# An encoder's MLP input: the last quarter turned by VectorE and transfers instead of TensorE

## Chip, cores and metric

The kernel runs on one core of a Trainium2 chip. The metric is the device time in microseconds of one execution; the median of three runs is taken.

## The reference, cut to what matters

Two layers; each has attention heads, an output projection that is added to the residual `h` (256 tokens x 2048), and an MLP. All arithmetic is float32.

```python
h = h + concatenate([mix, cross], axis=-1) @ w_o[i]          # 2048 -> 2048
n = rms_norm(h, mlp_norm[i])
h = h + square(relu(n @ w_up[i])) @ w_down[i]                # 2048 -> 8192 -> 2048
```

The up product needs the normed input with its features on the partitions, while `h` has tokens on the partitions. So the MLP's input must be transposed: 16 blocks `k` of 128 features by 256 tokens.

## The kernel before

**Exactness.** Each float32 operand is split into a rounded part hi and the rest lo (`split`, L505: ScalarE writes hi at L507, VectorE writes lo at L508), and a product is three matmuls: hi by hi, hi by lo, lo by hi (`products`, L399, the matmul at L411, 256 tokens as the moving side).

**Order.** The program is a list of grains, each one a step of TensorE with stages `load`, `lift`, `pre`, `prep` that are written some grains ahead (`ahead`). Within an engine the order is set afterwards by a planner that simulates the timeline. `tc.issue_after(ins)` puts the instructions of a block that go to the engine of `ins` behind it on that engine; `past(fn, pair)` does so for a ScalarE and a VectorE instruction; `later(n, ...)` writes a piece n grains later. Every engine and each DMA queue runs in order.

**Output projection and MLP input.** The projection comes in four blocks of 512 columns. After each of the first three, `o_done` adds it to `h`; after the third it takes a provisional scale from three quarters of the squares (`guard`), and quarters 0 to 2 of the MLP's input (4 blocks `k` each) go this way: ScalarE scales (`scaled`, L962), VectorE transposes 32 x 32 blocks within the partitions (`far_blocks`, L626), four transfers on SP's queue move the blocks to their partitions (L629, 128 KB each), and `arrived` applies the gain and splits (`split_pair`: ScalarE L537, VectorE L538) into `hT`. The last quarter can be finished only when the fourth block of the projection is summed: L1005 adds its two PSUM tiles to the scaled residual `y` (`begun`), and TensorE transposes `y` in eight 128 x 128 pieces (`transposed`, L525, matmuls with the identity into `pt_n`), from which L537 and L538 write `hT`. `box["ready"]` is the last pair of them; the add of the fourth block to `h` (L985) comes behind it.

**The up stage.** `up_grains` makes one chunk `m` of 128 of the 8192 columns: a 1 MB load into `raw_U` (L1045, two buffers, SP's queue), and two halves of eight `k` each, split apart (tiles `uh`, `ul`, two buffers). The first four chunks (`LEAD`) come before the first down product, so 4 x 48 = 192 matmuls. Numbering the halves 0 to 7, halves 2 and 4 lie in `u_b` (tag `b`, three buffers, shared with the down weights), half 5 in `u_th`, `u_tl` (later the down product's `th`, `tl`), the others in `uh`, `ul`. Before, the four chunks run one after the other, each with all of its 16 `k`. Halves of chunks 1 and 2 are written behind `box["summed"]`, the last sum of L1005. The chunks' sums lie in the PSUM pool `acc` of four banks, which the projection's last tiles use too. `squared` follows each chunk.

**The first down step** loads `b` (L1154, SP), and its lift copies a piece into a tile `t` of tag `T` (two buffers; ScalarE L1165), adds by a GpSimd transfer (L1166), and VectorE adds three more (L1172 to L1174); `th`, `tl` are split from it. `h_s`, the scaled quarter 2, and `y` are in tag `T` too.

## Time and profile before

| | |
|---|---|
| median of three runs | 1991.65 us (1991.28 to 1991.91) |
| the profiled execution | 1992.31 us, span 1990.5 us |
| TensorE clock granted | 0.999 of full speed |
| first up matmul to first down matmul, layer 0 | 419.24 to 442.84 us |
| the same, layer 1 | 1323.35 to 1346.07 us |

Times inside the profile count from the start of the span. PE is TensorE, PEld its weight loads, DVE VectorE, ACT ScalarE, POOL GpSimd, and SPq, POOLq are the instructions that issue transfers. A timeline row has the start, the duration (merged over the count at its end), engine, line, operation, written and read tiles; in brackets is the idle time before it and what ended that. A group's row ends with busy time, mean ns of one, and the idle time before. Matmuls are pipelined, so that the duration of one is longer than the slot that it takes; the chain of waits gives the slots.

### The profile page before, as it was taken

The numbers are of one execution on the slowest core, as the hardware profiler recorded it, in microseconds if no ns is written. First come the engines' busy times: TensorE is split into PE (matmuls) and PEld (weight loads), VectorE is DVE, ScalarE is ACT, GpSimd is POOL, SyncE is SP. The second block draws the span as 40 slices with busy tenths as digits, with TensorE's granted clock in tenths as the row PEclk, the third lists the DMA queues.
The fourth block names the chain that finished last, engine by engine and source line by source line (L and its number), as shares of the span: only waits on it lengthen the run. The fifth ranks groups of instructions, "written<-read, shape, count | busy, mean of one in ns | idle before, by whom it ended". The sixth has DMA issues, their size and how long they took to land.

```text
span 1990.5 us, 33096 instructions
## 1 busy us (share of the span) xinstructions
PE 1980.6 (100%) x12832; PEld 1799.3 (90%) x12832; DVE 1725.6 (87%) x2096; ACT 1442.2 (72%) x2105; POOL 149.9 (8%) x205
## 2 busy tenths in 40 slices
PE   9999999999999999999999999999999999999998
PEld 8999999899999999999998888889999999999997
DVE  6777767589999999999999879779999999999997
ACT  6755555577887778877887657668788777877786
POOL 0000000000000000000001001000000000000001
PEclk9999999999999999999999999999999999999999
DMA  7855655767777777777778765667777777777775
GB/s 289 320 193 208 199 192 184 271 198 248 222 231 237 229 232 237 222 239 235 222 229 223 267 221 171 220 202 249 238 222 229 236 229 229 237 229 241 228 225 156
DMA packets 110685, 452.46 MB, mean 227 GB/s; under 512 B 18880, under 2 KB 40640, under 8 KB 63168
## 3 DMA queue, kind: packets, MB, share of 16 engines
q1 hardware_dynamic: 90144, 413.38, 60.7%
q0 software_dynamic: 20096, 36.45, 10.5%
q8 instruction: 100, 1.64, 0.3%
q10 hardware_dynamic: 288, 0.52, 0.1%
q14 instruction: 57, 0.47, 0.1%
HBM read 397.78 MB, written 4.19 MB: 202 GB/s over the span
## 4 chain that ended last, share of the span: by engine, by line
PE 97%; ACT 1%; DVE 1%; DMA 1%; issue 0%; DVEq 0%; SPq 0%; POOLq 0%; POOL 0%; ACTq 0%
PE ps_u L411 35%; PE p L1195 10%; PE p L1199 10%; PE p L1198 10%; PE ps_s L411 9%; PE ps_m L391 7%; PE ps_m L392 7%; PE ps_m L388 7%; DMA first<-in_x 0%; ACT sq L856 0%; PE sc_ps L604 0%; PE sc_ps L605 0%; PE sc_ps L603 0%; PE av L696 0%; PE av L697 0%
## 5 line engine op out<-in xcount | busy, mean ns | idle before, releaser
L411 PE MATMUL ps_u<-hT,uh 128*128 128x256 f32 x3874 | 674.6, 276 | 0.0
L411 PEld LDWEIGHTS ps_u<-hT,uh 128*128 128x128 f32 x3874 | 588.5, 188 | 5.8
L411 PE MATMUL ps_u<-hT,ul 128*128 128x256 f32 x1994 | 550.7, 276 | 0.0
L507 ACT ACTIVATE uh<-raw_U 128x1024 fp32r<-128x1024 f32 x262 | 277.6, 1061 | 153.8 <-PE ps_u L411 150.7
L411 PEld LDWEIGHTS ps_u<-hT,ul 128*128 128x128 f32 x1994 | 374.3, 188 | 0.0
L507 ACT ACTIVATE hi<-raw 128x1024 fp32r<-128x1024 f32 (+1 forms) x215 | 222.0, 1036 | 182.2 <-PE ps_m L392 93.3
L508 DVE TENSOR_TENSOR lo<-raw,hi 128x1024 fp32r<-128x1024 f32 (+1 forms) x215 | 255.3, 1191 | 109.2 <-ACT hi L507 108.5
L508 DVE TENSOR_TENSOR ul<-raw_U,uh 128x1024 fp32r<-128x1024 f32 x262 | 319.8, 1221 | 14.2 <-ACT uh L507 14.1
L508 DVE TENSOR_TENSOR tl<-t,th 128x2048 fp32r<-128x2048 f32 x120 | 274.8, 2290 | 51.1 <-ACT th L507 50.9
L507 ACT ACTIVATE th<-t 128x2048 fp32r<-128x2048 f32 x120 | 230.9, 1924 | 90.4 <-PE p L1199 90.4
L508 DVE TENSOR_TENSOR bl<-b,bh 128x1536 fp32r<-128x1536 f32 x120 | 210.3, 1753 | 0.3 <-ACT bh L507 0.3
L1166 POOL DMA_DIRECT2D t<-b x120 | 104.2, 868 | 1159.3 <-ACT t L1165 1103.4
L1195 PE MATMUL p<-th,a_s 128*128 128x512 f32 x480 | 187.4, 391 | 0.0
L1198 PE MATMUL p<-tl,a_s 128*128 128x512 f32 x480 | 187.2, 390 | 0.0
L1199 PE MATMUL p<-th,a_s 128*128 128x512 f32 x480 | 186.7, 389 | 0.0
L507 ACT ACTIVATE bh<-b 128x1536 fp32r<-128x1536 f32 x120 | 178.7, 1489 | 3.5
L411 PE MATMUL ps_s<-nT,hi 128*128 128x256 f32 x896 | 154.6, 277 | 0.0
L1199 PE MATMUL p<-bh,a_s 128*128 128x512 f32 x360 | 140.9, 391 | 0.0
L1198 PE MATMUL p<-bl,a_s 128*128 128x512 f32 x360 | 140.1, 389 | 0.0
L1195 PE MATMUL p<-bh,a_s 128*128 128x512 f32 x360 | 140.1, 389 | 0.0
L411 PEld LDWEIGHTS ps_s<-nT,hi 128*128 128x128 f32 x896 | 135.3, 188 | 0.2
L411 PE MATMUL ps_s<-nT,lo 128*128 128x256 f32 x448 | 124.2, 277 | 0.0
(293 smaller groups left out, 3639.2 us busy)
## 6 DMA issues: line engine op xcount, KB each, us to landing
raw_U<-in_w_up SPq DMA_DIRECT2D x128, 1024.0 KB, 6.3
b<-in_w_pair SPq DMA_DIRECT2D x120, 1024.0 KB, 5.8
raw<-in_w_o SPq DMA_DIRECT2D x32, 1024.0 KB, 4.9
t<-b POOLq DMA_DIRECT2D x120, 256.0 KB, 6.5
raw<-in_w_b SPq DMA_DIRECT2D x21, 1024.0 KB, 5.5
raw<-in_w_av SPq DMA_DIRECT2D x12, 1024.0 KB, 5.1
raw<-in_w_aq SPq DMA_DIRECT2D x12, 1024.0 KB, 4.9
raw<-in_w_ak SPq DMA_DIRECT2D x12, 1024.0 KB, 4.9
```

Of the source, the lines that this page charges most:

```text
L388: first = nc.tensor.matmul(ps, ah, hi[:, s], start=st, stop=False)
L391: nc.tensor.matmul(ps, ah, lo[:, s], start=False, stop=False)
L392: final = nc.tensor.matmul(ps, al, hi[:, s], start=False, stop=sp)
L411: ins = nc.tensor.matmul(ps, x, acts[:, k, part], start=k == n == 0, stop=k == KT - 1 and n == 2)
L507: first = nc.scalar.activation(dst_hi, src, AF.Copy)
L508: return first, nc.vector.tensor_tensor(dst_lo, src, dst_hi.bitcast(F32), op=ALU.subtract)
L1166: nc.gpsimd.dma_start(s[:, 3, :], b[:, 1, :], accum_op=ALU.add)
L1195: ins = nc.tensor.matmul(ps, a[:, 0, ai, :], hi[:, s], start=entered, stop=False, skip_group_check=True)
L1198: nc.tensor.matmul(ps, a[:, 0, ai, :], lo[:, s], start=False, stop=False, skip_group_check=True)
L1199: nc.tensor.matmul(ps, a[:, 1, ai, :], hi[:, s], start=False, stop=ends, skip_group_check=True)
```

## The change

In both layers, `far_blocks` with the new `summed` replaces `transposed` for the last quarter: VectorE sums a tile and turns it, twice, and four transfers on SP's queue bring the blocks. The target is `y` and the blocks lie in `box["still"]`, the scaled quarter 2. `box["summed"]` is now the second of these transposes.

Chunks 0, 1 and 2 first do their `k` 0 to 11, and their last quarters follow chunk 2's third, in the order 0, 1, 2; then chunk 3 with all 16. Chunk 2's sum goes to the PSUM pool `att`. Halves 6 and 7 get rooms of their own (`u_z`), which are the later tiles `z0`, `z1`, now opened with the first down step. Half 2 is written earlier and no longer behind the sums; chunk 2's halves are written behind the last split before them.

```diff
@@ products
+        return ins
@@ far_blocks
-            nc.vector.transpose(blocks[:, :, i].rearrange("p b k j -> p k b j"),
-                                src(i).rearrange("p (k n b) -> p k b n", k=4, b=4))
+            box["turned"] = nc.vector.transpose(blocks[:, :, i].rearrange("p b k j -> p k b j"),
+                                                src(i).rearrange("p (k n b) -> p k b n", k=4, b=4))
@@ arrived
-            split_pair(dst, raw[:, :, :, n], which, k0 + n, by_quarters=True)
+            last = split_pair(dst, raw[:, :, :, n], which, k0 + n, by_quarters=True)
+        return last
@@ o_done, scaled
+            box["still"] = y
@@ o_done, nb == 3
-                for i in range(NT):
-                    box["summed"] = nc.vector.scalar_tensor_tensor(y[:, i, :], w.ps[i], box["scale"][:, i : i + 1],
-                                                                   y[:, i, :], op0=ALU.mult, op1=ALU.add)
-                box["ready"] = transposed(box["hT"], lambda i, k: y[:, i, k % 4 * P : (k % 4 + 1) * P],
-                                          list(range(12, KT)), (G_M0, G_M1)[layer])
+                def summed(i):
+                    nc.vector.scalar_tensor_tensor(y[:, i, :], w.ps[i], box["scale"][:, i : i + 1], y[:, i, :],
+                                                   op0=ALU.mult, op1=ALU.add)
+                    return y[:, i, :]
+
+                raw = far_blocks(summed, (box["still"], y.rearrange("p t c -> p (t c)")))
+                box["summed"] = box["turned"]
+                box["ready"] = arrived(box["hT"], raw, 12, (G_M0, G_M1)[layer])
@@ up_grains, prep and prepared
-            with tc.issue_after(box["summed"].ins) if m in (1, 2) else nullcontext():
+            if m == 2:
+                past(lambda: prepared(hf), box["splits"][-1])
+                return
+            with tc.issue_after(box["summed"].ins) if m == hf == 1 else nullcontext():
                 prepared(hf)
...
-            if lead and (half in (2, 4) or half > 4 and half % 3 == 2):
+            if lead and half in (2, 4, 5, 6, 7):
...
+                elif half > 5:
+                    room = at.mlp.tile([P, 2, HALF], F32R, tag=f"z{hf}", name="u_z")
+                    own[hf] = room[:, 0], room[:, 1]
@@ up_grains, run
-                box["z"] = [at.mlp.tile([P, 4, 512], F32, tag=f"z{q}", name=f"z{q}") for q in range(2)]
-                box["z_set"] = set()
...
-                    own["ps"] = at.acc.tile([P, 512], F32, tag="acc", name="ps_u")[:, :SEQ]
+                    pool, tag, bufs = (at.att, "att", at.banks) if m == 2 else (at.acc, "acc", None)
+                    own["ps"] = pool.tile([P, 512], F32, tag=tag, bufs=bufs, name="ps_u")[:, :SEQ]
...
+            acts = box["hT0" if lead else "hT"]
+            if m < 3 and hf == 1:
+                hi, lo = own.pop(hf)
+                last = products(own["ps"], acts, KT // 2, KT // 4, hi, lo)
+                box.setdefault("rests", []).append((m, own["ps"], hi[:, HALF // 2 :], lo[:, HALF // 2 :]))
+                if m == 2:
+                    for other, ps, hi, lo in box.pop("rests"):
+                        with tc.issue_after(last.ins):
+                            last = products(ps, acts, KT * 3 // 4, KT // 4, hi, lo)
+                        squared(layer, other, ps)
+                return
...
-            squared(layer, m, own["ps"])
-
-        soon = (8, 8, 3) if m == 1 else SOONER
+            if m > 2:
+                squared(layer, m, own["ps"])
+
+        early = (8, 8, 6)
-        return [Grain(lambda: run(0), None, load, None, lambda: prep(0), soon),
-                Grain(lambda: run(1), after, None, None, lambda: prep(1), SOONER)]
+        return [Grain(lambda: run(0), None, load, None, lambda: prep(0), early if m < 2 else SOONER),
+                Grain(lambda: run(1), after, None, None, lambda: prep(1), early if m == 0 else SOONER)]
@@ down_grains, run, first step
+                box["z"] = [at.mlp.tile([P, 4, 512], F32, tag=f"z{q}", name=f"z{q}") for q in range(2)]
+                box["z_set"] = set()
```

More of the change, by code (lines that the diff above doesn't have):

```diff
@@ L1090, in run @@
                 if lead:
-                    own["ps"] = at.acc.tile([P, 512], F32, tag="acc", name="ps_u")[:, :SEQ]
+                    pool, tag, bufs = (at.att, "att", at.banks) if m == 2 else (at.acc, "acc", None)
+                    own["ps"] = pool.tile([P, 512], F32, tag=tag, bufs=bufs, name="ps_u")[:, :SEQ]
                 else:
                     own["ps"] = sum_of("up")[:, :SEQ]
+            acts = box["hT0" if lead else "hT"]
[9 more added lines that the diff above has]
+                return
             with tc.issue_after(box["late"].ins) if m == hf == 0 else nullcontext():
-                products(own["ps"], box["hT0" if lead else "hT"], hf * (KT // 2), KT // 2, *own.pop(hf),
+                products(own["ps"], acts, hf * (KT // 2), KT // 2, *own.pop(hf),
                          keep_order=not lead, first=own.pop("first", None))
         def after():
-            squared(layer, m, own["ps"])
-        soon = (8, 8, 3) if m == 1 else SOONER
-        return [Grain(lambda: run(0), None, load, None, lambda: prep(0), soon),
-                Grain(lambda: run(1), after, None, None, lambda: prep(1), SOONER)]
+            if m > 2:
[3 more added lines that the diff above has]
+                Grain(lambda: run(1), after, None, None, lambda: prep(1), early if m == 0 else SOONER)]
     def squared(layer, m, ps):
```

## Prediction

> **What bounds the kernel now.** I read the page first: busy time, then the chain that ended last.

> ```profile
> span 1990.5 us, 33096 instructions
> PE 1980.6 (100%) x12832; PEld 1799.3 (90%) x12832; DVE 1725.6 (87%) x2096; ACT 1442.2 (72%) x2105; POOL 149.9 (8%) x205
> PE 97%; ACT 1%; DVE 1%; DMA 1%; issue 0%; DVEq 0%; SPq 0%; POOLq 0%; POOL 0%; ACTq 0%
> ```

> TensorE is busy all the time and carries 97% of the chain. So only two things can change the time: matmul slots that TensorE no longer executes, and new waits of TensorE. Next comes the chain inside the two stages that the change touches, from the last output-projection product to the first down product (second column: microseconds on the chain).

> ```profile
> 419.40 2.07 PE ps_u L411 x18
> 421.47 0.26 PE pt_n L525 x2
> 421.74 0.81 PE ps_u L411 x7
> 422.55 0.66 PE pt_n L525 x6
> 423.20 19.80 PE ps_u L411 x167
> ...
> 1323.51 2.08 PE ps_u L411 x18
> 1325.59 0.22 PE pt_n L525 x2
> 1325.81 0.83 PE ps_u L411 x7
> 1326.63 0.66 PE pt_n L525 x6
> 1327.29 18.94 PE ps_u L411 x167
> 1346.23 0.23 PE p L1195
> ```

> Both stages are an unbroken run of up matmuls (192) with eight transposes between them. Nothing else stands on the chain: no transfer and no VectorE wait. The same 167 matmuls take 19.80 us in layer 0 and 18.94 us in layer 1, so 118.6 and 113.4 ns a slot; that 0.86 us is the only slack besides the transposes.

> **The change, part by part.**

> *Transposes removed.* The chain gives 0.26 + 0.66 = 0.92 us in layer 0 and 0.22 + 0.66 = 0.88 us in layer 1. Term: -1.80 us.

> ```profile
> L525 PE MATMUL pt_n<-ident,h_s x16: 270/272/315, 421.3 to 1327.0; 128*128 128x128 f32 x16
> ```

> The duration of one (272 ns) is not its price; six in a row cost 0.66 us, 110 ns each, since they are pipelined. (The row's first start differs from the chain's by the drain of the matmul before.) [...]

> *What replaces them, and when it arrives.* Per layer: two VectorE block transposes, each after its sum, then four transfers on SP's queue, then the four ScalarE/VectorE pairs that also ran before, now reading SBUF. The same route already carries the quarter before it, so its rows price every step.

> ```profile
> 410.16 2.09 DVE L626 STREAM_TRANSPOSE h_t<-h_s 128x512 f32<-128x512 f32 x2 [1.86 <-DMA h_t<-h_t]
> 412.32 2.59 SPq L629 DMA_DIRECT2D h_s<-h_t  x4
> 418.35 1.71 ACT L537 ACTIVATE hT<-h_s,first 128x256 fp32r<-128x256 f32 x4 [2.71 <-DMA h_s<-h_t]
> 418.89 1.69 DVE L538 SCALAR_TENSOR_TENSOR hT<-h_s,first,hT 128x256 fp32r<-128x256 f32 x4 [1.23 <-ACT hT L537]
> 420.50 1.40 DVE L1005 SCALAR_TENSOR_TENSOR h_s<-ps_m,scale,h_s 128x512 f32<-128x512 f32 x2
> ...
> 1313.88 2.10 DVE L626 STREAM_TRANSPOSE h_t<-h_s 128x512 f32<-128x512 f32 x2 [1.47 <-DMA h_t<-h_t]
> 1321.00 1.71 ACT L537 ACTIVATE hT<-h_s,first 128x256 fp32r<-128x256 f32 x4 [1.65 <-DMA h_s<-h_t]
> 1323.15 1.40 DVE L1005 SCALAR_TENSOR_TENSOR h_s<-ps_m,scale,h_s 128x512 f32<-128x512 f32 x2
> ```

> From the end of the transposes to the first use of their data: 418.35 - 412.25 = 6.10 us in layer 0, 1321.00 - 1315.98 = 5.02 us in layer 1. Layer 0 in the new kernel: sums and transposes 420.50 + 1.40 + 2.09 = 423.99; data at 429.0 to 430.1; first hi and lo written about 1.0 us later (ScalarE's start to VectorE's start is 0.54 us, one VectorE step 0.42 us), 430.0 to 431.1; the fourth 1.3 us after that. TensorE needs it after three chunks' first three quarters, 3 x 36 = 108 matmuls: 419.40 + 108 x 0.1134 = 431.65 (432.2 at the slower pace), the fourth step 1.0 us later. Margin: 0.3 to 1.6 us. Layer 1: sums start at 1323.15, before the up stage; first pair at 1332.7 to 1333.8; needed at 1323.51 + 12.25 = 1335.76; margin 2 to 3 us. So the new wait costs TensorE nothing by these rows; without that cover it costs every microsecond by which the transfer is later. Bounds: 0 (no gain, since no wait stands on the chain now), and 2 us in layer 0, if the landing is late by once more the spread of these rows (1.1 us) and one weight split (1.2 us) stands in front of it, less 0.3 us of margin. I take 0, since both layers' rows put the data ahead of the need.

> *Order of chunks: weights earlier.* The rests at the end mean that the halves of chunks 1 and 2 are wanted after 36, 60, 72 and 96 matmuls instead of 48, 72, 96, 120; chunk 3 still after 144.

> ```profile
> 405.06 1.04 ACT L507 ACTIVATE u_b<-raw_U 128x1024 fp32r<-128x1024 f32 x1
> 421.81 2.35 DVE L508 TENSOR_TENSOR u_b<-raw_U,u_b 128x1024 fp32r<-128x1024 f32 x2
> 424.75 1.23 DVE L508 TENSOR_TENSOR u_tl<-raw_U,u_th 128x1024 fp32r<-128x1024 f32 x1 [0.58 <-ACT u_th L507]
> 425.89 1.22 DVE L508 TENSOR_TENSOR ul<-raw_U,uh 128x1024 fp32r<-128x1024 f32 x1
> ```

> VectorE queues halves 3, 4, 5 behind the second transpose: ready at 425.2, 426.4, 427.6 (1.2 us each), wanted at 426.2, 427.6, 430.3. Half 2 loses its place behind the sums; ScalarE's part of it ran at 405.06, and VectorE idles 1.86 us before 410.16, so it fits earlier; if it ended behind the transposes (425.2, wanted at 423.5) it would cost 1.7 us. I take 0. In layer 1 each margin is over a microsecond wider. VectorE gains 2.1 us per stage (two transposes); the row of its stage is:

> ```profile
> 419.20:443.00 23.80, 23.80 (x202) 23.64 (x201) 19.50 (x29) 14.50 (x26) 1.84 (x2) 1.00 0.84 290
> ```

> 19.50 of 23.80 us (third column) leaves 4.3 us, so the added work lies beside TensorE.

> *SP's queue.* Four issues (2.59 us) stand among the weight loads.

> ```profile
> 418.32 0.34 SPq L1154 DMA_DIRECT2D b<-in_w_pair  x1
> 423.13 0.63 ACT L1165 ACTIVATE t<-b 128x512 f32<-128x512 f32 x1 [2.12 <-DMA b<-in_w_pair]
> 426.00 1.46 SPq L1045 DMA_DIRECT2D raw_U<-in_w_up  x2
> 434.06 0.31 ACT L1077 ACTIVATE u<-raw_U 128x128 fp32r<-128x128 f32 x1 [1.80 <-DMA raw_U<-in_w_up]
> ```

> If they go first (424.0 to 426.6), chunk 3's load, which wants a raw buffer that half 3 or half 5 frees (425.2 or later), moves from 426.0 to at most 427.6. A load alone takes 423.13 - 418.32 = 4.8 us; with both splits (1.04 + 1.22) half 6 is ready by 434.7, wanted at 419.40 + 144 x 0.1134 = 435.7. Cost 0; one microsecond of cover.

> *Moved pieces.* The T buffers are held until the blocks land, so the first down step's lift (ScalarE copy, GpSimd accumulating transfer, three VectorE adds) goes from 423.13 to about 430.

> ```profile
> L1166 POOL DMA_DIRECT2D t<-b x120 | 104.2, 868 | 1159.3 <-ACT t L1165 1103.4
> t<-b POOLq DMA_DIRECT2D x120, 256.0 KB, 6.5
> 430.40 1.28 DVE L985 TENSOR_TENSOR first<-ps_m,first 128x512 f32<-128x512 f32 x2
> 444.15 1.91 ACT L507 ACTIVATE th<-t 128x2048 fp32r<-128x2048 f32 x1
> ```

> It then lands at 430 + 0.6 + 0.9 + 6.5 = 438, and its reader ran at 444.15: hidden. GpSimd's queue holds nothing else there. The add of the last output block (1.3 us behind the last pair, so by 434) frees the bank for chunk 3 at 435.7; chunk 2 no longer waits for it, having another pool's bank. The z tiles change place only.

> **Sum.** The profiled execution took 1992.31 us, 1.8 above its span and 0.66 above the median. 1992.31 - 1.80 = 1990.5; against the median, 1991.65 - 1.80 = 1989.85, so 1989.9.

> **Rivals.**
> (a) *Layer 0 also gets layer 1's pace.* The 4% slower slots follow the transposes in layer 0 but not in layer 1; the tiles are the same, so the pace looks set by how the stream is entered. Gain 0.86 more: 1989.0.
> (b) *The quarter lands late.* Layer 0's 0.3 us at worst is thin. If SP issues one weight load in front, the blocks come up to 4.8 us later and TensorE waits 3 to 4 us: 1989.9 + 3 to 4 = 1993 to 1994; a wait under a microsecond, 1990 to 1991. Against it: raw buffers are free only at 425.2.
> (c) *Slower.* Both loads stand in front, in both layers. The second of the two loads issued from 426.0 on was awaited until 434.06; blocks behind it, with their four issues (2.6 us) and the first pair (1.0 us), are usable at 437.7, against 431.65: 6.0 us. With two microseconds less in layer 1, 4.0 us: 1991.65 + 10.0 - 1.8 = 1999.9. It counts as slower from 5.8 us of waiting on. [...]
> (d) *Each transpose holds TensorE for its 272 ns.* 16 x 272 ns = 4.35 us: 1987.3, just faster. The chain's 110 ns speak against it.

> **How the numbers follow.** A change within 0.2%, 4.0 us here, can't be told from none. Forecast (1989.3 to 1990.6) 0.50, (a) 0.17, (b) 0.24, (c) 0.06, (d) 0.03. Faster is (d), slower is (c), the rest is the same. The range from 1988.6 to 1993.2 takes in (a), the forecast and most of (b).

> **What would show it.** Right: no TensorE row that reads the identity in either stage; the stage from first up to first down matmul shorter by 0.9 us in each layer; no idle TensorE ahead of the rests; the block transposes at about 424 and 1326.6, four SP issues straight behind. Wrong: TensorE released by ScalarE's or VectorE's write of the last quarter, or by a raw load; SP's weight load between the transposes and the block transfers; half 2's lo behind the transposes.

## The result: slower by 0.4%

The changed kernel took 1999.70 us (median of six runs, 1999.00 to 2001.02), the kernel before on the same chip 1991.47 us (1990.65 to 1991.94). The ratio is 1.0042 [1.0031, 1.0053]; the forecast was 1989.9 us. The profiled execution of the changed kernel took 2001.02 us, with a span of 1999.2 us.

The profile after, first the page (busy time and the shares of the chain), then TensorE's waits (engine, line, releaser: us in total, times, longest).

```profile
span 1999.2 us, 33086 instructions
PE 1982.6 (99%) x12816; PEld 1798.9 (90%) x12816; DVE 1730.7 (87%) x2100; ACT 1442.4 (72%) x2105; POOL 152.0 (8%) x205
PE 94%; DVE 2%; DMA 2%; ACT 1%; issue 1%; SPq 0%; DVEq 0%; POOLq 0%; POOL 0%; ACTq 0%
```

```profile
PE p L1221 <- ACT a_s L508: 5.7, 2, 3.5
PE p L1225 <- DVE a_s L509: 1.1, 4, 0.4
```

TensorE runs 16 instructions fewer, and two long waits have come in. Both are of the first down product (line 1221), for the hi part of `a_s`: the split sums of the first pair's activations. A comparison of the two traces gives the place of every microsecond (starts of the matmuls, in us):

| | layer 0 before | after | layer 1 before | after |
|---|---|---|---|---|
| first to last up matmul of the stage | 23.49 | 21.84 | 22.60 | 21.84 |
| last up to first down matmul | 0.12 | 3.74 | 0.12 | 2.54 |
| the first nine down matmuls | 2.09 | 4.14 | 2.09 | 3.96 |

From the first up matmul of layer 0 to that of layer 1 the kernel lost 4.81 us (-1.65 + 3.62 + 2.05 and 0.79 later), from there to the end 4.27 us (-0.76 + 2.42 + 1.87 and 0.74 later); 0.38 us was gained ahead of the first stage. Part of what is called later are matmuls that still ran at the lower clock shown below. The sum is the 8.7 us between the spans. So the stage that the prediction worked out did become shorter, and more than all of it was lost right behind it, in the wait and the nine matmuls after the wait.

The chain of waits of the changed kernel in layer 0, from the four issues behind the block transposes to `a_s` (start, us, what):

```profile
424.08 0.61 SPq L630
...
426.74 0.61 SPq L1052
...
427.39 0.50 SPq L1178
...
427.94 11.01 DMA raw_U<-in_w_up
...
438.97 1.06 ACT uh L508
440.03 0.31 ACT c L1138
440.33 0.20 ACT u L1090
440.53 0.96 ACT uh L508
...
441.52 1.23 DVE ul L509
442.74 0.35 DVE c L1147
...
443.11 0.30 DVE c L1148
...
443.44 0.96 ACT a_s L508
```

It leaves TensorE altogether. SP issues the four block transfers, chunk 3's raw load (426.74), 1 MB of down weights (427.39) and only then chunk 4's raw load, which lands 11.01 us later. ScalarE splits it (`uh`, 438.97), and only behind that squares chunk 1 (L1138, 440.03); VectorE writes the second half's lo (`ul`, 441.52) and only behind that the sums of the squares (L1147, L1148), which `a_s` is split from at 443.44. Nothing in that product needs chunk 4. Layer 1 has the same chain; there the load lands 11.42 us after its issue. ScalarE's queue in the timeline of the same kernel shows the blockage:

```profile
429.30 1.71 ACT L538 ACTIVATE hT<-h_s,first 128x256 fp32r<-128x256 f32 x4 [4.64 <-DMA h_s<-h_s]
...
432.51 2.02 ACT L508 ACTIVATE u_z<-raw_U 128x1024 fp32r<-128x1024 f32 x2 [0.67 <-DMA raw_U<-in_w_up]
434.43 1.47 ACT L508 ACTIVATE bh<-b 128x1536 fp32r<-128x1536 f32 x1
...
437.22 0.36 ACT L1137 ACTIVATE c<-ps_u 128x256 f32<-128x256 f32 x1
438.97 1.06 ACT L508 ACTIVATE uh<-raw_U 128x1024 fp32r<-128x1024 f32 x1 [1.38 <-DMA raw_U<-in_w_up]
439.93 0.40 ACT L1138 ACTIVATE c<-c 128x256 f32<-128x256 f32 x1
```

Chunk 1's relu (L1137) is done at 437.6; its square is free to run, but stands behind a split that idles 1.38 us for a load.

Behind the wait comes a second loss. The busy time by stretches (length, then PE, PEld, DVE, ACT and POOL with their counts, then the granted TensorE clock, the DMA share and GB/s) of the changed kernel:

```profile
440.70:444.40 3.70, 0.28 (x3) 0.08 (x1) 2.64 (x5) 2.43 (x5) 0.00 (x0) 1.00 1.06 345
444.40:445.70 1.30, 0.87 (x3) 0.43 (x4) 1.28 (x2) 1.30 (x2) 0.00 (x0) 1.00 1.03 422
445.70:449.10 3.40, 3.40 (x10) 2.72 (x11) 3.33 (x4) 1.35 (x3) 0.00 (x0) 0.51 1.01 429
449.10:452.00 2.90, 2.90 (x27) 2.90 (x27) 2.52 (x3) 2.87 (x6) 0.00 (x0) 0.99 0.09 34
```

TensorE comes back at full clock, 1.3 us later the granted clock falls to half (0.51 in the third row), and 3.4 us later it is back. At half clock a down matmul takes 0.43 us on the chain instead of 0.23.

### The profile page after: what moved, and what is told of

The parts are those of the page before. It is cut to its first block, busy times and chain, and to the rows that moved or that the text cites. A ratio compares the mean times of both kernels' runs of the same rounds, so it can differ in the third digit from the quotient of the medians.

```text
span 1999.2 us, 33086 instructions
## 1 busy us (share of the span) xinstructions
PE 1982.6 (99%) x12816; PEld 1798.9 (90%) x12816; DVE 1730.7 (87%) x2100; ACT 1442.4 (72%) x2105; POOL 152.0 (8%) x205
## 3 DMA queue, kind: packets, MB, share of 16 engines
q8 instruction: 100, 1.64, 0.3%
## 4 chain that ended last, share of the span: by engine, by line
PE 94%; DVE 2%; DMA 2%; ACT 1%; issue 1%; SPq 0%; DVEq 0%; POOLq 0%; POOL 0%; ACTq 0%
PE ps_u L411 33%; PE p L1225 10%; PE p L1221 9%; PE p L1224 9%; PE ps_s L411 9%; PE ps_m L391 7%; PE ps_m L392 7%; PE ps_m L388 7%; DMA raw_U<-in_w_up 1%; ACT uh L508 0%; DVE ul L509 0%; SPq L630 0%; ACT hi L508 0%; PE sc_ps L605 0%; PE sc_ps L606 0%
## 5 line engine op out<-in xcount | busy, mean ns | idle before, releaser
L411 PE MATMUL ps_u<-hT,uh 128*128 128x256 f32 x3812 | 662.7, 276 | 0.0
L411 PEld LDWEIGHTS ps_u<-hT,uh 128*128 128x128 f32 x3812 | 579.1, 188 | 5.8
L411 PE MATMUL ps_u<-hT,ul 128*128 128x256 f32 x1964 | 542.7, 276 | 0.0
L508 ACT ACTIVATE uh<-raw_U 128x1024 fp32r<-128x1024 f32 x258 | 273.5, 1061 | 157.1 <-PE ps_u L411 152.6
L411 PEld LDWEIGHTS ps_u<-hT,ul 128*128 128x128 f32 x1964 | 369.0, 188 | 0.0
L508 ACT ACTIVATE hi<-raw 128x1024 fp32r<-128x1024 f32 (+1 forms) x215 | 222.0, 1037 | 186.9 <-PE ps_m L392 96.5
L509 DVE TENSOR_TENSOR ul<-raw_U,uh 128x1024 fp32r<-128x1024 f32 x258 | 314.2, 1219 | 15.3 <-ACT uh L508 15.1
L508 ACT ACTIVATE th<-t 128x2048 fp32r<-128x2048 f32 x120 | 230.8, 1923 | 91.3 <-PE p L1225 91.3
L1190 POOL DMA_DIRECT2D t<-b x120 | 104.2, 869 | 1168.4 <-ACT t L1189 1091.4
L508 ACT ACTIVATE bh<-b 128x1536 fp32r<-128x1536 f32 x120 | 178.7, 1490 | 7.6 <-PE p L1225 3.9
L411 PE MATMUL ps_s<-nT,hi 128*128 128x256 f32 x896 | 154.6, 277 | 0.0
L411 PEld LDWEIGHTS ps_s<-nT,hi 128*128 128x128 f32 x896 | 135.4, 188 | 0.2
L411 PE MATMUL ps_s<-nT,lo 128*128 128x256 f32 x448 | 124.2, 277 | 0.0
## 6 DMA issues: line engine op xcount, KB each, us to landing
t<-b POOLq DMA_DIRECT2D x120, 256.0 KB, 6.6
```

What stands on the lines that cost most here:

```text
L411: ins = nc.tensor.matmul(ps, x, acts[:, k, part], start=k == n == 0, stop=k == KT - 1 and n == 2)
L508: first = nc.scalar.activation(dst_hi, src, AF.Copy)
L509: return first, nc.vector.tensor_tensor(dst_lo, src, dst_hi.bitcast(F32), op=ALU.subtract)
L1190: nc.gpsimd.dma_start(s[:, 3, :], b[:, 1, :], accum_op=ALU.add)
```

## The experiments

All are compared with the kernel before on the same chip. The theory after the comparison: `a_s` is late because chunk 4's split stands in front of its parts on ScalarE and VectorE, and the lower clock that follows the idle adds to the loss. The rivals: the new chunk order itself costs the time; the place of the load in SP's queue is the cause; the slow matmuls are slow for another reason than the idle. Experiments 5 and 6 ask why the split stands there.

**1. The splits put behind.** Chunk 4's split goes behind that of `a_s` on both engines; SP's queue stays.

```diff
+            if m == LEAD:
+                past(lambda: prepared(hf), box["a_pair", 0])
+                return
...
-            box["made", pair] = split(a[:, 0], a[:, 1], c[:, 1:])[1]
+            box["a_pair", pair] = split(a[:, 0], a[:, 1], c[:, 1:])
+            box["made", pair] = box["a_pair", pair][1]
```

> The changed kernel, with the split of chunk 4's two halves queued behind the split of the first down step's left side (a_s) on ScalarE and VectorE. The loads on SP keep their order. Theory 1 (the wait is ScalarE's and VectorE's queue order: a split that waits for a late load stands in front of the square and the sums): a_s is ready at about 440.4 in layer 0, the first down matmul follows chunk 3 at about 440.8, at most 0.3 us of waits for the lo part and for chunk 4's ul remain, 1989 to 1991 us. Rival (the late load itself holds everything): chunk 4 now waits for its split as long as the first down step did before, 1997 to 2000 us.

Measured: 1989.38 us, ratio 0.9991 [0.9982, 1.0000]. The timeline of this kernel, ScalarE and then TensorE:

```profile
438.16 0.95 ACT L508 ACTIVATE a_s<-c 128x896 fp32r<-128x896 f32 x1 [0.68 <-DVE c L1151]
439.01 1.04 ACT L508 ACTIVATE uh<-raw_U 128x1024 fp32r<-128x1024 f32 x1
```

```profile
440.39 0.40 PE L411 MATMUL ps_u<-hT_l,u_z 128*128 128x256 f32 x2
440.62 0.40 PE L1225 MATMUL p<-bh,a_s 128*128 128x512 f32 x1
440.86 0.40 PE L1228 MATMUL p<-bl,a_s 128*128 128x512 f32 x1
```

`a_s` comes at 438.16, the first down matmul at 440.62 without idle time before it, and the nine behind it take 2.09 us. First up to first down matmul is 21.96 us in both layers, against 23.61 and 22.72 before: 2.41 us less. This one edit takes away the whole loss. The new order of chunks stays in this kernel, so the order by itself isn't what costs the time. The same edit, timed again:

> The changed kernel with chunk 4's split halves queued behind the split of a_s, timed again for a narrower interval. Theory: both stages take 21.96 us from first up to first down matmul, against 23.61 and 22.72 before, so 2.4 us less than before: a ratio of 0.9988. Rival: what the stages gain is given back later in the layers, and the ratio is 1.000.

Measured: 1989.88 us, ratio 0.9992 [0.9984, 1.0001]. The point agrees with the theory; the interval doesn't exclude 1. In this profile one wait of 0.6 us for the lo of `a_s` is left. Both timings lie 1.5 to 2.1 us below the kernel before.

**2. The load put ahead.** SP issues the down weights of step 1 behind chunk 4's raw load; the splits stay where they were.

```diff
-            nc.sync.dma_start(own["b"].rearrange("p a b -> p (a b)"),
-                              t[f"w_pair{layer}"][j * 2 + q])
+            with tc.issue_after(box["up_load", LEAD].ins) if n == 1 else nullcontext():
+                nc.sync.dma_start(own["b"].rearrange("p a b -> p (a b)"),
+                                  t[f"w_pair{layer}"][j * 2 + q])
```

> The changed kernel, with the down load of step 1 queued behind chunk 4's raw load on SP. Theory 1: chunk 4's load lands about 3.4 us earlier (435.5 in layer 0); ScalarE's copy for step 1's lift then waits for the down load until about 439, so a_s comes at about 442.5 and a wait of 1 to 2 us remains: 1993 to 1997 us, by whether the clock still drops. Rival (the order of the two loads does not matter, the 2 to 3 us of block transfers in front of both do): 1999 to 2000 us.

Measured: 1993.30 us, 1.0009 [1.0000, 1.0018]. SP's timeline, TensorE's waits and two stretches behind the first down matmul (layer 0, layer 1):

```profile
425.66 1.17 SPq L1052 DMA_DIRECT2D raw_U<-in_w_up  x2
426.88 2.65 SPq L1180 DMA_DIRECT2D b<-in_w_pair  x2
```

```profile
PE p L1223 <- ACT a_s L508: 1.7, 2, 1.2
PE p L1227 <- DVE a_s L509: 0.8, 2, 0.4
```

```profile
443.00:446.40 3.40, 3.40 (x12) 2.83 (x11) 3.33 (x4) 1.49 (x3) 0.00 (x0) 0.51 1.05 413
1346.80:1350.00 3.20, 2.78 (x12) 2.03 (x13) 3.13 (x5) 2.46 (x4) 0.00 (x0) 1.00 1.05 351
```

ScalarE first reads chunk 4's load at 434.67 and doesn't idle for it. The block transfers still go ahead of both raw loads, so they alone didn't make that load late; the down weights between the two loads did most of it, and the rival falls. The waits for the hi fall from 5.7 to 1.7 us in all, but don't go: the splits stand in front of the sums, whenever their load lands. In layer 0 the wait of 1.2 us is followed by half clock for 3.4 us (0.51 in the first stretch); in layer 1 the wait of half a microsecond isn't (1.00 in the second). The load's place is what made the wait long, the split's place what made it a wait.

**3. Both.**

```diff
+ the edits of 1 and 2
```

> The changed kernel with both edits: chunk 4's split halves queued behind the split of a_s, and the down load of step 1 behind chunk 4's raw load. Theory: once a_s no longer stands behind chunk 4's split, when chunk 4's load lands doesn't matter, so the second edit adds nothing: within 2 us of the kernel with the first edit alone (1989.4), unless the later down load now holds up something on ScalarE ahead of the squares; its copy of that load stands in front of chunk 1's square, which would show as a wait of about 0.7 us of the first down matmul in layer 0 and no lower clock behind it: 1989 to 1991. Rival: the load order is a cause of its own, worth the 3 us a layer that it brought alone: below 1988.

Measured: 1993.15 us, 1.0010 [1.0000, 1.0019]: not below 1988, so the rival falls, but also 3.3 us above the first edit alone (1989.88 us, timed along with it), where at most 2 were expected. TensorE's waits for `a_s` make up 2.6 us of that (0.8 for the hi, 1.8 for the lo). The chain and ScalarE's and TensorE's timeline of this kernel:

```profile
427.03 10.79 DMA b<-in_w_pair
```

```profile
437.91 0.63 ACT L1195 ACTIVATE t<-b 128x512 f32<-128x512 f32 x1 [2.15 <-DMA b<-in_w_pair]
438.44 0.40 ACT L1142 ACTIVATE c<-c 128x256 f32<-128x256 f32 x1
```

```profile
440.99 0.50 PE L1227 MATMUL p<-bh,a_s 128*128 128x512 f32 x1 [0.85 <-ACT a_s L508]
442.12 0.50 PE L1231 MATMUL p<-bh,a_s 128*128 128x512 f32 x1 [0.40 <-DVE a_s L509]
```

Now the down weights are last of the three loads and land 10.79 us after their issue, as chunk 4's load did before; and now it is the copy of the lift (L1195) that idles on ScalarE in front of a square. In both kernels the load that stands last is late, and the first thing on ScalarE that reads it holds up `a_s`. Behind the idle of 0.85 and 0.40 us the granted clock stays at full speed (1.00 from 439.00 to 446.00).

**4. TensorE kept busy in the wait.** Sixteen (layer 0) and eleven (layer 1) matmuls of ones into an unused PSUM bank stand between the last up and the first down matmul; all else as in the changed kernel.

```diff
+                for _ in range((16, 11)[layer]):
+                    with tc.issue_after(last.ins):
+                        last = nc.tensor.matmul(room[:, :P], ones, ones, start=True, stop=True)
```

> The changed kernel with 16 (layer 0) and 11 (layer 1) idle matmuls of ones by ones behind chunk 3, in the wait ahead of the first down matmul; the wait itself stays. If the slow matmuls behind the wait (0.43 us a slot instead of 0.23) are the clock's answer to TensorE's idling, they run at the full rate: 2.2 us less in each layer, 1995 to 1996 us. If they are slow because of other traffic at that time (VectorE, the transfers), nothing changes: 1999 to 2000 us.

Measured: 1996.34 us, 1.0025 [1.0015, 1.0034], 3.4 us less than the changed kernel, where 4.4 had been expected. A stretch of this kernel behind the first down matmul (444.25):

```profile
444.20:449.20 5.00, 4.95 (x34) 4.60 (x35) 4.90 (x7) 1.97 (x4) 0.00 (x0) 1.00 0.86 357
```

The first down matmul is as late as it was (25.84 us behind the first up matmul, against 25.58), but the clock stays at 1.00 and the nine behind it take 2.15 us instead of 4.14. So the slow matmuls come from the idle time, and the wait and the clock are two losses: some 3.4 us of the 8.2 are the clock's.

**5. The rooms alone.** The kernel before with one part of the change: halves 6 and 7 in the rooms `u_z`.

```diff
-            if lead and (half in (2, 4) or half > 4 and half % 3 == 2):
+            if lead and half in (2, 4, 5, 6, 7):
...
+                elif half > 5:
+                    room = at.mlp.tile([P, 2, HALF], F32R, tag=f"z{hf}", name="u_z")
+                    own[hf] = room[:, 0], room[:, 1]
```

> The kernel before with one part of the change: halves 6 and 7 get the rooms u_z, which leaves the two rooms uh, ul free for chunk 4. Theory: these rooms are what lets chunk 4's split stand in front of the first pair's squares; before, it had to wait until chunk 3 was done with uh, ul. So both halves of chunk 4's split now run in front of the squares on ScalarE (from about 434, with the raw load that landed at 434.06) instead of behind the split of a_s (440.37). Since SP's queue is as before and that load is early, a_s comes only some 1 to 2 us later than 439.5, still in time or with a wait under 1 us: 1991 to 1993. Rival: the place of the split is set by other parts of the change (the later squares): it stays behind a_s, and the time is that of before, 1991.4, with a_s at 439.5.

Measured: 1992.53 us, 1.0004 [0.9995, 1.0013]. ScalarE's timeline, first in the kernel before (where it also did the small copy `u` of chunk 4 at 434.06), then in this one:

```profile
439.51 0.95 ACT L507 ACTIVATE a_s<-c 128x896 fp32r<-128x896 f32 x1 [0.59 <-DVE c L1124]
440.37 1.04 ACT L507 ACTIVATE uh<-raw_U 128x1024 fp32r<-128x1024 f32 x1
```

```profile
433.98 1.05 ACT L507 ACTIVATE uh<-raw_U 128x1024 fp32r<-128x1024 f32 x1
434.93 0.30 ACT L1080 ACTIVATE u<-raw_U 128x128 fp32r<-128x128 f32 x1
435.13 1.05 ACT L507 ACTIVATE uh<-raw_U 128x1024 fp32r<-128x1024 f32 x1
...
438.93 0.95 ACT L507 ACTIVATE a_s<-c 128x896 fp32r<-128x896 f32 x1 [0.43 <-DVE c L1125]
```

In the kernel before chunk 4's split ran behind `a_s`; with nothing but the new rooms both its halves run in front, before the squares. So the rooms move it. And it costs nothing here: SP issues chunk 4's load right behind chunk 3's, it is there by 434, and `a_s` comes at 438.93, without any wait of TensorE in the stage.

**6. The rooms taken back.** The changed kernel with halves 6 and 7 in `uh`, `ul`.

```diff
-            if lead and half in (2, 4, 5, 6, 7):
+            if lead and half in (2, 4, 5):
...
-                elif half > 5:
-                    room = at.mlp.tile([P, 2, HALF], F32R, tag=f"z{hf}", name="u_z")
-                    own[hf] = room[:, 0], room[:, 1]
```

> The changed kernel with halves 6 and 7 back in the rooms uh, ul; the block transposes, the order of chunks and everything else as changed. Theory: without the free rooms chunk 4's split can't run before chunk 3 has done with its half 6 (about 438.6), and stands behind the squares; only the small copy u of chunk 4 still waits for the late raw load in front of two of them. a_s comes 1 to 2 us earlier than in the changed kernel (443.4): a wait of 1 to 2 us in layer 0 with the lower clock behind it, half that in layer 1: 1993 to 1997. Rival: the rooms don't matter, the late load alone does: a_s at 443 as in the changed kernel, 1999 to 2000.

Measured: 1998.55 us, 1.0033 [1.0021, 1.0046]: above the range, for another reason. ScalarE's and TensorE's timeline in this kernel:

```profile
434.54 0.63 ACT L1186 ACTIVATE t<-b 128x512 f32<-128x512 f32 x1 [4.15 <-DMA b<-in_w_pair]
435.08 1.04 ACT L508 ACTIVATE uh<-raw_U 128x1024 fp32r<-128x1024 f32 x1
...
441.73 1.06 ACT L508 ACTIVATE uh<-raw_U 128x1024 fp32r<-128x1024 f32 x1 [1.36 <-PE ps_u L411]
```

```profile
436.17 0.50 PE L411 MATMUL ps_u<-hT,uh 128*128 128x256 f32 x2 [1.93 <-ACT uh L508]
```

The place came out as expected: chunk 4's split waits for TensorE to be done with half 6 and runs at 441.73, behind the squares. But now the copy of the lift (L1186) idles 4.15 us for its down weights in front of half 6's split, and TensorE waits 1.93 us for the hi and 0.76 us for the lo ahead of chunk 3, with half clock behind them until 441.0 (0.83 over 440.00 to 443.00; the up matmuls start 0.21 us apart there, and 0.11 us after it). It is the same fault with another reader in front. In neither layer does the first down matmul wait for the hi of `a_s`, but that says little, since chunk 3 itself is late: counted from the first up matmul, `a_s` comes 24.97 us later in layer 0 (24.58 in the changed kernel) and 22.40 us later in layer 1 (23.38). The sums were done at 441.49, and the split that waits for TensorE still stands between them and `a_s` (442.69). So this run doesn't show that the rooms are needed for the loss.

**7. The new order alone.** TensorE's transposes are kept, the chunks run in the new order.

```diff
-                raw = far_blocks(summed, (box["still"], y.rearrange("p t c -> p (t c)")))
-                box["summed"] = box["turned"]
-                box["ready"] = arrived(box["hT"], raw, 12, (G_M0, G_M1)[layer])
+                box["ready"] = transposed(box["hT"], lambda i, k: y[:, i, k % 4 * P : (k % 4 + 1) * P],
+                                          list(range(12, KT)), (G_M0, G_M1)[layer])
```

> The change without its transposes by blocks: TensorE still transposes the last quarter, but chunks 0 to 2 take their last quarters at the end, as in the changed kernel. Theory 1 (the four block transfers and a down load push chunk 4's raw load back on SP's queue, so that ScalarE's split of it stands in front of chunk 1's square): without the block transfers and the VectorE transposes all raw loads are issued 2 to 3 us earlier, chunk 4's load lands by about 434.5, the first down matmul waits for nothing, and the time is that of before, 1991 to 1992 us. Rival (the new order of chunks alone makes the squares late): the wait of 2 to 4 us ahead of the first down matmul stays in both layers, 1997 to 2000 us.

Measured: 2002.05 us, 1.0055 [1.0040, 1.0070]: neither. TensorE's waits and its timeline in this kernel:

```profile
PE ps_u L411 <- DVE hT L539: 7.6, 2, 4.7
```

```profile
431.25 0.98 PE L411 MATMUL ps_u<-hT,u_b 128*128 128x256 f32 x3 [2.87 <-DVE hT L539]
```

The loss lies elsewhere: chunk 2's sum takes a bank of the pool `att`, which the transposes' `pt_n` use in this kernel, so TensorE waits for the splits that read them, 2.87 and 4.73 us, and each time the clock falls to half (0.50 over 432.00 to 434.00 and over 1346.40 to 1350.40). The first down matmul waits for nothing here, but chunk 3 is late too. That run was a poor test of the theory; it shows only that the order, with chunk 2's sum in this pool, can't be had without the other part.

**8. The block transposes alone.** The old order and the old buffers.

```diff
- the new order of chunks, the bank of chunk 2, the rooms u_z, the lead of half 2
```

> The block transposes and transfers alone; the chunks in the order of before, each with all of its k, and every other buffer as before. Theory: the new chunk order is what gives the transfers their cover. In this order chunk 2's sum needs a PSUM bank that is freed only by the add of the last output block, which comes behind the last quarter's splits; TensorE so has three quarters of chunks 0 and 1 (72 matmuls, 8.2 us, to about 427.6 in layer 0) and the quarter comes at about 430: a wait of 2 to 3 us in layer 0 and 0.5 to 1 in layer 1, with a lower granted clock behind the longer one (2 us lost): 1993 to 1998. The first down matmul waits for nothing new, since the squares of chunks 0 and 1 are made early again. Rival: the order of the chunks is what costs the time and the transfers need no cover: no wait ahead of the last quarters, 1989 to 1991.

Measured: 1994.68 us, 1.0016 [1.0007, 1.0025]. TensorE's waits in this kernel:

```profile
PE ps_u L411 <- ACT hT L537: 2.6, 2, 1.3
PE ps_u L411 <- DVE u_b L508: 1.6, 1, 1.6
```

TensorE waits for the quarter 1.3 us in each layer: without the new order the transfers aren't covered. The total lies in the expected range by other terms than expected: the wait in layer 0 is shorter because TensorE is already late when it comes, no lower clock follows (1.00 from 421.00 to 432.00), and 1.6 us are spent on half 2's lo (`u_b`), written behind the two transposes. That is the 1.7 us which the prediction gave for just this, if half 2 isn't moved ahead.

## Why the prediction was wrong, step by step

*Right: the transposes' price.* The stage's up part is 21.84 us in both layers, 114.3 ns a matmul. Layer 1 gained 0.76 us (0.88 predicted); layer 0 gained 1.65 us, that is its 0.92 and 0.73 of rival (a)'s 0.86. The changed kernel, without the transposes, runs chunks 0 to 2 at 113.3 ns a matmul in both layers, and so does experiment 3 in layer 0. Of the kernels with them, the kernel before has the slower pace in layer 0 (118.6 ns) and experiment 7 has it there for part of the stage (117.7 ns from 435.41 to 441.06), while in layer 1 neither the kernel before (113.4 ns) nor experiment 5 has it (97 matmuls in 11.00 us). So the transposes alone don't explain it, and its cause stays open. Rival (d)'s 272 ns each fell.

*Right: arrival and weights.* ScalarE read the quarter at 429.30 (429.0 to 430.1 predicted) and at 1336.54, 8.76 us behind layer 1's first up matmul; TensorE's first rest ran at 431.14 without a wait. The half-2 step came out as taken. None of the signs listed as wrong was there. Of those listed as right one failed: from first up to first down matmul the stage became 1.97 us longer in layer 0 and 1.66 us longer in layer 1, not 0.9 us shorter. The others were there. No sign of either list named what could come between the last up and the first down matmul.

*Failed: "SP's queue".* The step followed the load of chunk 3, which was in time (`u_z` at 432.51, hi of both halves by 434.5, against 434.7 for half 6). It did not follow the next load in the same queue, chunk 4's, whose landing it had quoted: ScalarE's 1.80 us of idle at 434.06, in front of the copy `u`, is the wait for it. With four block transfers, chunk 3's load and 1 MB of down weights ahead of it, that load landed at 438.95. Experiment 2 shows that the down weights made most of the difference. In every kernel with the new order of chunks that doesn't move them they come between the two raw loads (experiments 6 and 7 too); with the rooms alone (5) or the block transfers alone (8) they come behind both. So the step looked for the four new issues, and what it missed was that the order of the loads changes. "Cost 0; one microsecond of cover" was the cover of the other load.

*Failed: "Moved pieces".* "The z tiles change place only" passed over what the new rooms set free: `uh` and `ul`, which chunk 4's split can now take before chunk 3 is done. Experiment 5 shows it move from behind `a_s` to the front of the squares. The step also left out `squared` of chunks 0 and 1: ScalarE's first relu began at 436.50 instead of 431.90, so the squares fell in with the split. Neither cost anything by itself: the moved split with an early load gives `a_s` at 438.93 (experiment 5), the late squares and the late load with the split behind give 438.16 (experiment 1). Together with the late load, the wait of the first down matmul is 3.6 us in layer 0 and 2.4 us in layer 1. The early squares with the moved split and the late load weren't tried, since chunks 0 and 1 need their rests first; so the share of the late squares stays open.

*Not priced: what an idle TensorE does next.* The prediction gave each wait its own length. Here a wait was followed by half clock, which cost some 3.4 us over both layers (experiment 4).

Rival (c)'s 1999.9 us is near the measured time by accident: in its mechanism the blocks land behind the raw loads and TensorE waits for the quarter, and the blocks were issued first and landed in time. It had the right resource, SP's queue, and the wrong victim.

## What to carry to other kernels

When a change puts transfers into a queue, or reorders the steps that fill it, follow every load in it to its first reader, and then what stands behind that reader on its own engine: a split that idles for its load (1.38 us in the changed kernel) holds up work that has nothing to do with it. A buffer set free is a change of order too: ask which later piece can now run early, and what it will stand in front of. The cure was one edit of the order on ScalarE and VectorE, not on the queue that was late.

## What the runs showed of the hardware

In the changed kernel TensorE's two long waits for the hi of `a_s` (5.7 us together, 3.5 us the longer) were each followed by half clock, for 3.41 us. The fall isn't tied to the moment at which work begins again: in the changed kernel it came 1.3 us after that (445.75 against 444.44), in experiment 7 before it (430.6, while TensorE waited until 431.25).

```profile
439.53:442.94 3.41, 1.77 (x10) 1.09 (x10) 2.27 (x5) 2.49 (x3) 0.00 (x0) 1.00 1.02 359
```

```profile
438.93:442.34 3.41, 2.05 (x18) 1.85 (x16) 2.25 (x3) 3.20 (x6) 0.00 (x0) 1.00 1.03 371
442.34:445.75 3.41, 0.92 (x3) 0.48 (x4) 2.36 (x5) 2.31 (x3) 0.00 (x0) 1.00 1.06 369
1350.29:1353.70 3.41, 1.14 (x4) 0.66 (x5) 2.36 (x5) 2.54 (x3) 0.00 (x0) 1.00 1.05 373
1988.58:1991.99 3.41, 2.13 (x18) 1.93 (x17) 3.38 (x10) 1.23 (x4) 0.00 (x0) 1.00 0.59 222
```

In the first TensorE idled 1.64 us, and the next step ran at half clock. In the others it idled 1.36, 2.49, 2.27 and 1.28 us; half clock followed the 2.49 and the 2.27 us, and full clock the 1.36 and the 1.28 us. Between 1.36 and 1.64 us these stretches show nothing.

Of the other traces only the waits stand here. Half clock followed 2.87 and 4.73 us (experiment 7), and 1.93 and 0.76 us close together (experiment 6, layer 0). It did not follow 0.85 and 0.40 us (experiment 3), 0.47 and 0.76 us (experiment 6, layer 1), or 1.60 us and then 1.32 us in layer 0 and 1.25 us in layer 1 of experiment 8. So the length of the longest wait doesn't tell the two apart: behind the 1.60 us of experiment 8 the clock stayed at 1.00, and in experiment 2, whose longest wait is 1.2 us, it fell. From half clock it went back after 3.4 us, but in layer 1 of experiment 7 it was at half for longer, over all of 1346.40 to 1350.40 (0.50). The idle is taken from the profile's matmul times, whose ends are modelled.

All transfers of SP's queue landed in the order of their issue, 594 in the kernel before and 602 in the changed kernel, and so did the 152 of GpSimd's queue in each.
